# Expert rows summed into x in HBM by accumulating scatters, the last expert's rows and the down biases by products

## The chip, the cores and the metric

One Trainium2 chip, one core. The metric is device time in microseconds (us). Before the change the median of 3 runs is 2022.94 us (2020.0 to 2031.31).

## The reference, cut to what matters

One layer over 512 latent tokens of 1024 channels. The part that the change touches is the mixture of experts at its end and the norm behind it:

```python
logits = (xf @ lp['router_w'] + lp['router_b']).astype(jnp.float32)
top_v, top_e = lax.top_k(logits, TOP_K)            # 4 of 32 experts per token
weights = jax.nn.softmax(top_v, axis=-1)
...                                                # per expert e, on its tokens' rows
return clamped_swiglu(gate, up) @ lp['exp_w_down'][e] + lp['exp_b_down'][e]
...
contrib = yb[dest] * sorted_w[:, None].astype(yb.dtype)
out = jax.ops.segment_sum(contrib, sorted_tok, num_segments=n_tok)
...
x = x + ga2 * moe_ffn(h, lp)                       # then one final RMSNorm
```

`ga2` is a row of 1024 numbers. 512 tokens times 4 choices over 32 experts is 64 rows per expert on average; the kernel gives every expert 128 slots.

## The kernel before, in words

**Routing.** `project_out` ends the mixer: its four tiles of 128 tokens are added to `xn` and written to `d_xn` in HBM. In front of it `merge` makes the operand `mL` on POOL, one subtraction for each of 8 blocks (L1164), and PE waits for each. `route_tile` and `route` then find each token's experts and its slot in each.

**The experts.** `expert_chain` walks a list `seq` in an order written out by hand for PE, ACT and DVE; SP and POOL stand as a scheduler puts them. Round `r` has 12 blocks: 4 of the gate weights of expert r (`pos` 0 to 3), 4 of the down weights of expert r-1 (`pos` 4 to 7) and 4 of the up weights of expert r (`pos` 8 to 11); round 0 has no down part and round 32 nothing else. For each block SP loads 1 MB of weights into one of 6 buffers `raw` (L1462), ACT casts it to `wh` (L1480), DVE takes the remainder `wl` = raw - wh into one of 3 buffers (L1486), and PE multiplies 12 times by 512 columns (L1497, L1498, L1502). The casts run three blocks ahead, the remainders two. `bias_mm` (L1552) opens each gate and each up part, so its rows mark where a round starts.

**The tokens of an expert.** `gather_x` fetches the rows of experts 0 to 3 by products with one-hot matrices on PE (L1523), two experts at a time: the first pair ahead of round 0, the second within round 1. From expert 4 on, `x_rows` gathers 128 rows from `d_h2` by an indirect DMA on POOL (L1532), and `x_turn` transposes them in the round before they are used (L1544). That DMA needs `slots`, the token of each slot. `slot_table` makes it through HBM: 16 indirect scatters of token numbers into one table `d_tab` (L1418), and a load of the table (L1421). What builds the weights and tables runs as the generators `side` and `side_end`, a step behind each block.

**The end.** `y_out` copies an expert's product to `am` (L1589) and ACT's queue writes it to `d_y` (L1591). `finish` gathers each token's four rows back from `d_y` by 16 indirect DMAs on POOL (L1768). For each tile of 128 tokens PE sums two of them by products with diagonal matrices (L1778), the down biases (L1779) and the last expert's rows (L1780); DVE adds the other two (L1782, L1783), multiplies by `ga2` and adds `x` (L1787, L1788); `final_norm` follows and SP writes the tile out (L1810).

Of the kernel before, what the change touches and what calls it, by code (L numbers as in the profile page):

```python
# [19 lines left out]
NLAT = 512  # L20
# [11 lines left out]
NMM = 4  # L32
# [19 lines left out]
NLATE = C_IOTA1 + 128  # L52
# [14 lines left out]
def make_consts():  # L67
# [42 lines left out]
    l[:, C_EB:C_EB + 32] = 1024.0 * np.arange(32)  # L110
    hst = np.zeros((40, 512), np.float32)
# [41 lines left out]
class K:  # L153
# [1030 lines left out]
    def xn_load(self, pool):  # L1184
        self.xn = pool.tile([128, 4, 1024], F32, name="xn")
        self.nc.sync.dma_start(self.xn, self.A["x"].rearrange("(i p) d -> p i d", p=128))
        self.ga1 = self.row_tile(pool, "ga1", self.d_mod[0])

    def project_out(self, c, H, L, tiles=range(4)):
# [10 lines left out]
        if c == 3:  # L1200
            nc.sync.dma_start(self.d_xn[128 * i:128 * i + 128, :], self.xn[:, i, :])
# [117 lines left out]
    def counts(self, pool):  # L1319

        nc = self.nc
        nc.vector.tensor_scalar_add(self.pm, self.pm1, -1.0)
        pc = self.ps.tile([128, 32], F32, name="b1")
        ch = self.moe.tile([128, 4, 32], BF, name="ch")
        nc.vector.tensor_scalar(ch, self.pm, 0.0, None, op0=OP.is_ge)
        for j in range(4):
# [6 lines left out]
    def scratch(self, *shape):  # L1333

        t = self.mraw.tile([128, 2048], F32, name="raw", bufs=RAW)
        n = math.prod(shape)
        names = "abcd"[:len(shape)]
        return t[:, :n].rearrange(f"p ({' '.join(names)}) -> p {' '.join(names)}", **dict(zip(names, shape)))

    def weights(self, pool):  # L1340
# [7 lines left out]
        yield  # L1348
# [17 lines left out]
        nc.vector.tensor_reduce(e_, t, axis=mybir.AxisListType.X, op=OP.add)
        yield

        f = moe.tile([128, 4, 4], F32, name="dsf")
        nc.vector.tensor_sub(f, dst, e_)  # L1370
        big = moe.tile([128, 4, 4], F32, name="big")
# [3 lines left out]
        nc.vector.scalar_tensor_tensor(s, e_, 0.125, f, op0=OP.mult, op1=OP.add)  # L1375
        self.slot = pool.tile([128, 4, 4], I32, name="slot")
        nc.vector.scalar_tensor_tensor(self.slot, big, 8192.0, s, op0=OP.mult, op1=OP.add)
        self.slot_table(pool)
        self.f_, self.e_, self.big = f, e_, big

    def weights_end(self, pool):

        nc = self.nc
        moe = self.moe
        oh = self.oh
        f, e_, big = self.f_, self.e_, self.big
        self.keepR = self.mbL.tile([128, 4096], F32R, name="mL")
        self.keep = self.mb.tile([128, 4096], F32, name="mH")
        wl = moe.tile([128, 4, 4], F32, name="ex")
        nc.vector.tensor_mul(wl, self.wts, oh[:, :, :, NE - 1])  # L1390
        self.wlast = pool.tile([128, 4, 1], F32, name="wlast")
        nc.vector.tensor_reduce(self.wlast.rearrange("p a b -> p (a b)"), wl, axis=mybir.AxisListType.X, op=OP.add)
        yield
        yield from self.down_bias(pool, oh)
        yield
        self.wts2 = pool.tile([128, 4, 4], F32, name="wts2")
        nc.vector.tensor_mul(self.wts2, self.wts, big)
        nc.vector.tensor_sub(self.wts, self.wts, self.wts2)
        yield
        g = moe.tile([128, 4, 4], F32, name="dst")  # L1400
        nc.vector.tensor_scalar_min(g, f, 127.0)
        self.dsti = pool.tile([128, 4, 4], I32, name="dsti")
        nc.vector.scalar_tensor_tensor(g, e_, 0.125, g, op0=OP.mult, op1=OP.add)

        nc.vector.tensor_scalar_min(self.dsti, g, 128.0 * (NE - 1))
        nc.vector.tensor_scalar(g, f, 128.0, -128.0, op0=OP.max, op1=OP.add)
        self.dst2 = pool.tile([128, 4, 4], I32, name="dst2")
        nc.vector.scalar_tensor_tensor(self.dst2, e_, 0.375, g, op0=OP.mult, op1=OP.add)

    def slot_table(self, pool):  # L1410

        nc = self.nc
        tok = pool.tile([128, 4], I32, name="tok")
        lt = self.late[:, C_TOK:C_TOK + 12].rearrange("p (i c) -> p i c", c=3)
        nc.vector.tensor_add(tok.rearrange("p (i c) -> p i c", c=1), lt[:, :, 0:1], lt[:, :, 1:2])
        for i in range(4):
            for k in range(4):
                nc.gpsimd.indirect_dma_start(out=self.d_tab, out_offset=bass.IndirectOffsetOnAxis(ap=self.slot[:, i, k:k + 1], axis=0),  # L1418
                                             in_=tok[:, i:i + 1], in_offset=None, bounds_check=128 * NE - 1, oob_is_err=False)
        self.slots = pool.tile([128, NE], I32, name="slots")  # L1420
        nc.gpsimd.dma_start(self.slots, self.d_tab.rearrange("(e s) a -> s (e a)", s=128))  # L1421

    def down_bias(self, pool, oh):

        nc = self.nc
        moe = self.moe
        w = self.scratch(4, 3, 32)
        u = self.scratch(4, 4, 32)
# [125 lines left out]
    def gate_sig(self, E):  # L1554
# [5 lines left out]
        nc.scalar.activation(sg, sg, AF.Sigmoid, scale=-1.702, bias=self.eps[:, 5:6])  # L1560

# [5 lines left out]
    def up_clamp(self, E):  # L1567
        u = E["u"] = self.moe.tile([128, 1024], F32, name="sg")
        self.nc.vector.tensor_scalar(u, E["up"].rearrange("p a b -> p (a b)"), 7.0, -7.0, op0=OP.min, op1=OP.max)
        E["a"] = self.moe.tile([128, 8, 128], F32, name="am")  # L1570
# [16 lines left out]
    def y_out(self, E):  # L1587
        y = E["y"] = self.moe.tile([128, 1024], F32, name="am")
        self.nc.scalar.copy(y, E["dn"].rearrange("p a b -> p (a b)"))  # L1589
        if E["e"] < NE - 1:  # L1590
            self.nc.scalar.dma_start(self.d_y[128 * E["e"]:128 * E["e"] + 128, :], y)  # L1591

    def expert_bias(self, tmp, m):
# [14 lines left out]
        z = tmp.tile([128, 2, 32], F32, name="selz", bufs=1)  # L1608
# [5 lines left out]
        zi = tmp.tile([128, 32], I32, name="zi", bufs=1)  # L1614
        nc.gpsimd.memset(zi, 0)
        nc.sync.dma_start(self.d_tab.rearrange("(p e) a -> p (e a)", p=128), zi)

    def experts(self):
        self.xf, self.xg = [], {}
        self.nsplit = 0  # L1620
        ET = mybir.EngineType
        with self.tc.manual_schedule(engines={ET.PE, ET.Activation, ET.DVE}):
            y = self.expert_chain()
        self.finish(y)

    def side(self):

        self.counts(self.small)
        yield
        yield from self.weights(self.small)  # L1630

    def side_end(self):

        yield from self.weights_end(self.small)
        yield from self.last_table()

    def expert_chain(self):
# [423 lines left out]
```

## Time and profile before

| | us |
|---|---|
| median of 3 runs | 2022.94 |
| profiled execution, its own time | 2020.75 |
| its span, first to last instruction | 2019.0 |
| PE busy | 1910.1 |
| DVE busy | 1651.7 |
| ACT busy | 1253.7 |
| POOL busy | 328.8 |

The busy times are means over stages that are limited by different things. The expert rounds take the last 1230 us; the chain of waits, the timeline of one engine in a short window and the table of windows say what limits each stretch.

### The profile page before, as it was taken

How to read it: one execution, taken by the hardware profiler on the slowest of the kernel's cores; microseconds unless marked ns; L12 is line 12 of the kernel's file. 1: busy time of each engine (PE TensorE's matmuls, PEld its weight loads, DVE VectorE, ACT ScalarE, POOL GpSimd, SP SyncE). 2: the span in 40 equal slices, each digit the busy share in tenths (PEclk: the TensorE clock that was granted, in tenths of full speed). 3: DMA queues.
4: the chain of work that ended last, by engine and by line, in shares of the span. 5: the costliest groups of instructions: out<-in, count | busy, mean ns of one | idle time of the engine just before them, and what ended most of it. 6: DMA issues, size and time to landing. Idle time of an engine off the chain costs nothing.

```text
span 2019.0 us, 29040 instructions
## 1 busy us (share of the span) xinstructions
PE 1910.1 (95%) x11216; PEld 1500.3 (74%) x11216; DVE 1651.7 (82%) x1760; ACT 1253.7 (62%) x1464; POOL 328.8 (16%) x364
## 2 busy tenths in 40 slices
PE   7999878989999898988999999999999999999986
PEld 4767666667676697876888888888888888888863
DVE  5755786868785567897999999999999999999985
ACT  4522535454545435765777777777777777777762
POOL 0000515353523451220000000000000000000012
PEclk9999989989899998998999999999999999999998
DMA  9665233120111575988999999999999999999984
GB/s 319 205 201 190 85 100 106 56 65 30 52 51 50 181 249 180 343 327 319 365 375 384 372 393 376 373 383 371 387 382 373 385 370 392 370 375 388 369 340 167
DMA packets 154675, 545.11 MB, mean 270 GB/s; under 512 B 14442, under 2 KB 75626, under 8 KB 105379
## 3 DMA queue, kind: packets, MB, share of 16 engines
q1 hardware_dynamic: 140775, 497.97, 66.4%
q0 software_dynamic: 6928, 23.10, 3.4%
q10 hardware_dynamic: 6828, 22.13, 2.7%
q8 instruction: 90, 1.47, 0.3%
q14 instruction: 54, 0.44, 0.1%
HBM read 507.71 MB, written 35.43 MB: 269 GB/s over the span
## 4 chain that ended last, share of the span: by engine, by line
PE 69%; DVE 8%; DMA 3%; issue 2%; POOL 2%; ACT 2%; SPq 0%; POOLq 0%; DVEq 0%; ACTq 0%
PE gp L1497 6%; PE up L1497 6%; PE gp L1498 6%; PE up L1498 6%; PE up L1502 6%; PE gp L1502 6%; PE dn L1502 6%; PE dn L1498 6%; PE dn L1497 6%; PE fill L1091 2%; PE b L1580 1%; PE b L1544 1%; PE mm L870 1%; PE b L1523 1%; PE ch L911 1%
## 5 line engine op out<-in xcount | busy, mean ns | idle before, releaser
L1486 DVE TENSOR_TENSOR wl<-raw,wh 128x2048 fp32r<-128x2048 f32 x384 | 868.8, 2290 | 51.7 <-PE gp L1502 28.3
L1480 ACT CAST wh<-raw 128x2048 fp32r<-128x2048 f32 x384 | 720.8, 1905 | 95.7 <-PE gp L1498 63.5
L1497 PE MATMUL dn<-wh,aH 128*128 128x512 f32 x512 | 207.4, 405 | 0.4 <-ACT aH L1583 0.4
L1497 PE MATMUL gp<-wh,xH 128*128 128x512 f32 x512 | 204.7, 400 | 0.0
L1497 PE MATMUL up<-wh,xH 128*128 128x512 f32 x512 | 204.5, 399 | 0.0
L1498 PE MATMUL dn<-wh,aL 128*128 128x512 f32 x512 | 202.4, 395 | 1.5 <-DVE aL L1584 1.3
L1498 PE MATMUL gp<-wh,xL 128*128 128x512 f32 x512 | 201.9, 394 | 0.0
L1498 PE MATMUL up<-wh,xL 128*128 128x512 f32 x512 | 201.8, 394 | 0.0
L1532 POOL DMA_INDIRECT xg<-d_h,slots x28 | 26.3, 940 | 901.7 <-PE b L1544 893.3
L1502 PE MATMUL dn<-wl,aH 128*128 128x512 f32 x512 | 140.5, 396 | 0.0
L1502 PE MATMUL up<-wl,xH 128*128 128x512 f32 x512 | 139.2, 393 | 0.0
L1502 PE MATMUL gp<-wl,xH 128*128 128x512 f32 x512 | 139.0, 393 | 0.0
L1583 ACT CAST aH<-b 128x512 fp32r<-128x512 f32 x64 | 37.5, 586 | 134.5 <-PE b L1580 134.5
L1498 PEld LDWEIGHTS dn<-wh,aL 128*128 128x128 f32 x512 | 97.2, 190 | 21.8 <-DVE aL L1584 2.6
L1502 PEld LDWEIGHTS gp<-wl,xH 128*128 128x128 f32 x512 | 96.2, 188 | 22.9
L1502 PEld LDWEIGHTS up<-wl,xH 128*128 128x128 f32 x512 | 96.2, 188 | 22.9
L1502 PEld LDWEIGHTS dn<-wl,aH 128*128 128x128 f32 x512 | 97.1, 190 | 21.4
L1498 PEld LDWEIGHTS up<-wh,xL 128*128 128x128 f32 x512 | 96.6, 189 | 21.3
L1498 PEld LDWEIGHTS gp<-wh,xL 128*128 128x128 f32 x512 | 96.5, 189 | 21.1
L1497 PEld LDWEIGHTS dn<-wh,aH 128*128 128x128 f32 x512 | 97.1, 190 | 20.1 <-ACT aH L1583 0.8
L1497 PEld LDWEIGHTS gp<-wh,xH 128*128 128x128 f32 x512 | 96.4, 188 | 20.8
L1497 PEld LDWEIGHTS up<-wh,xH 128*128 128x128 f32 x512 | 96.4, 188 | 20.7
(512 smaller groups left out, 3708.2 us busy)
## 6 DMA issues: line engine op xcount, KB each, us to landing
raw<-in_exp_w_gate_dram SPq DMA_DIRECT2D x128, 1024.0 KB, 7.2
raw<-in_exp_w_up_dram SPq DMA_DIRECT2D x128, 1024.0 KB, 7.7
raw<-in_exp_w_down_dram SPq DMA_DIRECT2D x128, 1024.0 KB, 9.1
raw<-in_w_ada_dram SPq DMA_DIRECT2D x32, 512.0 KB, 4.5
d_y<-am ACTq DMA_DIRECT2D x31, 512.0 KB, 8.8
raw<-in_w_in_dram SPq DMA_DIRECT2D x24, 512.0 KB, 4.1
wa<-in_w_ada_dram SPq DMA_DIRECT2D x7, 1024.0 KB, 11.0
raw<-in_w_in_dram SPq DMA_DIRECT2D x6, 1024.0 KB, 5.5
```

What stands on the lines that cost most here:

```text
L870: nc.tensor.matmul(mm[:, d].rearrange("p a t -> p (a t)"), BK[:, d, ch[d], :], AZ[:, d].rearrange("p a t -> p (a t)"), start=True, stop=True)
L911: nc.tensor.matmul(sp[:, d, :], bk[:, d, :], uv[:, d, :], start=True, stop=True)
L1091: nc.tensor.matmul(ps, a[:, k, :], b[:, k, :], start=(n == 0), stop=(n == 23))
L1480: self.nc.scalar.copy(h, t)
L1486: self.nc.vector.tensor_sub(lo, t, h)
L1497: mm(ps[:, c, :], xH[:, k0 + kk, :], wh[:, cs], start=first and kk == 0, stop=False)
L1498: mm(ps[:, c, :], xL[:, k0 + kk, :], wh[:, cs], start=False, stop=False)
L1502: mm(ps[:, c, :], xH[:, k0 + kk, :], wl[:, cs], start=False, stop=last and kk == 1)
L1523: nc.tensor.matmul(ps[:, c].rearrange("p e s -> p (e s)"), src[:, 2 * q + c, 128 * i:128 * i + 128], oh[:, i].rearrange("p e s -> p (e s)" ...
L1532: self.nc.gpsimd.indirect_dma_start(out=t, out_offset=None, in_=self.d_h2, in_offset=bass.IndirectOffsetOnAxis(ap=self.slots[:, e:e + 1], ...
L1544: nc.tensor.transpose(pt[:, j, :], self.xg[e][:, 128 * k:128 * k + 128], self.ident)
L1583: nc.scalar.copy(aH, pt)
```

## The change

1. `d_xn` becomes `d_acc`, 128 rows longer. Each expert's rows but the last's are scaled by their slot's weight as they are copied (ACT, `y`), multiplied by `ga2` (POOL), and added to `d_acc` by an accumulating indirect scatter (POOL's queue). Empty slots add zero to the spare rows.
2. The slot tables carry token and weight, and are four, one for each of the four choices. They are made ahead of the first remainder `wl` (`places`), and summed within round 1 (`slot_rows`).
3. Only experts 0 and 1 are fetched by products. Experts 2 and 3 are gathered from HBM within round 1; gathers skip empty slots.
4. `finish` adds to the loaded `d_acc` only the bias product and the last expert's product, times `ga2`. The order of the end is written out by hand too.

```diff
-NMM = 4
+NMM = 2
     def xn_load(self, pool):
+        self.nc.gpsimd.dma_start(self.d_acc[NLAT:NLAT + 128, :], self.xn[:, 3, :])
...
-            nc.sync.dma_start(self.d_xn[128 * i:128 * i + 128, :], self.xn[:, i, :])
+            nc.sync.dma_start(self.d_acc[128 * i:128 * i + 128, :], self.xn[:, i, :])
...
+    def places(self, pool):          # was weights(), a step behind each block
...
+        for i in range(4):
+            for k in range(4):
+                nc.gpsimd.indirect_dma_start(out=self.d_tab[k], out_offset=bass.IndirectOffsetOnAxis(ap=slot[:, i, k:k + 1], axis=0),
+                                             in_=tw[:, i, k, :], in_offset=None, bounds_check=128 * NE - 1, oob_is_err=False)
+        self.tab = moe.tile([128, 4, NE, 2], F32, name="y")
+        for j, t in enumerate(self.d_tab):
+            nc.gpsimd.dma_start(self.tab[:, j], t.rearrange("(s e) a -> s e a", e=NE))
...
     def y_out(self, E):
-        y = E["y"] = self.moe.tile([128, 1024], F32, name="am")
-        self.nc.scalar.copy(y, E["dn"].rearrange("p a b -> p (a b)"))
-        if E["e"] < NE - 1:
-            self.nc.scalar.dma_start(self.d_y[128 * E["e"]:128 * E["e"] + 128, :], y)
+        if e == NE - 1:
+            for c in range(2):
+                cs = slice(512 * c, 512 * c + 512)
+                nc.vector.tensor_mul(y[:, cs], E["dn"][:, c, :], self.ga2[:, cs])
+            return
+        nc.scalar.activation(y, E["dn"].rearrange("p a b -> p (a b)"), AF.Copy, scale=self.wslot[:, e:e + 1])
+        nc.gpsimd.tensor_mul(y, y, self.ga2)
+        nc.gpsimd.indirect_dma_start(out=self.d_acc, out_offset=bass.IndirectOffsetOnAxis(ap=self.slotd[:, e:e + 1], axis=0), in_=y, in_offset=None, compute_op=OP.add)
...
-        nc.sync.dma_start(self.d_tab.rearrange("(p e) a -> p (e a)", p=128), zi)
+        for t in self.d_tab:
+            nc.gpsimd.dma_start(t.rearrange("(p e) a -> p (e a)", p=128), zi)
...
+        self.places(self.small)
+        low(0)
+        low(1)
...
+            if r == NE and pos == 4:
+                self.last_part(0, 0)
+                for h in range(2):
+                    self.up_clamp(P, slice(h, h + 1))
+                    self.up_half(P, h)
+                    if h == 0:
+                        self.turn(P, 0)
...
+    def sum_load(self):              # called in round 31 behind y_out
+        for i in range(4):
+            x = self.moex.tile([128, 1024], F32, name=("xH", "xL")[i % 2], bufs=XB)
+            self.nc.gpsimd.dma_start(x, self.d_acc[128 * i:128 * i + 128, :])
...
+    def last_part(self, i, j):
...
+            if j == 0:
+                nc.tensor.matmul(ps, self.wD[:, i, :], self.bD[:, cs], start=True, stop=False)
+            else:
+                nc.tensor.matmul(ps, self.wT[:, i, :], self.ylast[:, cs], start=False, stop=True)
...
+        def add(i):
+            for c in range(2):
+                cs = slice(512 * c, 512 * c + 512)
+                nc.vector.tensor_add(self.xf[i][:, cs], self.xf[i][:, cs], self.pss[i][c])
...
+        add(0); root(0); add(1); scaled(0); root(1); add(3); scaled(1); root(3); add(2); root(2); scaled(3); scaled(2)
```

(`root` is a tile's square sum and root on ACT, `scaled` its division, the product with the norm's weights and the write; the last line is twelve lines in the code.)

The order of instructions at three places, before and after. First POOL in the merge, where it makes `mL` for PE (`xn` adds follow). Before:

```order
L186 TENSOR_TENSOR yaL<-ya,yaH 128x512
L186 TENSOR_TENSOR wh<-raw,wh 128x1024
L1607 TENSOR_TENSOR bias<-biasf,biash 32x512 x2
L1164 TENSOR_TENSOR mL<-ga,mH 128x512 x8
L1199 TENSOR_TENSOR xn<-xn,mo 128x256 x5
```

After (L1191 writes the spare rows, L1639 zeroes a table each):

```order
L1629 TENSOR_TENSOR bias<-biasf,biash 32x512 x2
L1167 TENSOR_TENSOR mL<-ga,mH 128x512 x4
L1191 DMA d_acc<-xn 128x1024
L1637 MEMSET gy 128x64
L1167 TENSOR_TENSOR mL<-ga,mH 128x512
L1639 DMA d_tab_67<-gy 128x64
L1639 DMA d_tab_68<-gy 128x64
L1167 TENSOR_TENSOR mL<-ga,mH 128x512
L1639 DMA d_tab_69<-gy 128x64
L1639 DMA d_tab_70<-gy 128x64
L1167 TENSOR_TENSOR mL<-ga,mH 128x512 x2
```

Five DMA issues stand among the eight subtractions, four of them ahead of the last two. Next DVE where the experts start, from the one-hot matrix of the first pair (L1513) on. Before:

```order
L1513 TENSOR_TENSOR xg<-late,pm_8063 128x1024
L1486 TENSOR_TENSOR wl<-raw,wh 128x2048 x3
L1322 TENSOR_SCALAR pm<-pm_8063 128x128
L1325 TENSOR_SCALAR ch<-pm 128x128
L1329 TENSOR_REDUCE mc<-b_8209 128x1
L1331 CAST maxc<-mc 128x1
```

After, the end of `places` (`slot` and `tw` are what the scatters take):

```order
L1360 TENSOR_REDUCE sm<-ex 128x4
L1361 RECIPROCAL sm<-sm 128x4
L1363 TENSOR_TENSOR wts<-ex,sm 128x16
L1366 TENSOR_TENSOR dsf<-dst,dse 128x16
L1368 TENSOR_SCALAR big<-dsf 128x16
L1371 TENSOR_SCALAR dst<-dsf 128x16
L1372 SCALAR_TENSOR_TENSOR dst<-dse,dst 128x16
L1374 SCALAR_TENSOR_TENSOR slot<-big,dst 128x16
L1377 COPY tw<-wts 128x16
L1379 TENSOR_TENSOR sm<-late 128x4
L1380 TENSOR_SCALAR tw<-sm 128x16
L1493 TENSOR_TENSOR wl<-raw,wh 128x2048 x3
```

Seventeen instructions now stand between the one-hot matrix and the first `wl`: these eleven, and six before them. Last PE behind the last up block, where the last down part (`dn`) begins. Before:

```order
L1502 MATMUL up<-wl,xH 128x512 x4
L1778 MATMUL gp<-raw,mH 128x512 x2
L1580 MATMUL b_16969<-first,am 128x128 x4
L1779 MATMUL gp<-mL 128x512
L1497 MATMUL dn<-wh,aH 128x512
```

After:

```order
L1509 MATMUL up<-wl,xH 128x512 x4
L1793 MATMUL gp<-mL 128x512 x2
L1594 MATMUL b_17012<-first,am 128x128 x4
L1504 MATMUL dn<-wh,aH 128x512
L1505 MATMUL dn<-wh,aL 128x512
```

The products with gathered rows (L1778) no longer stand ahead of the transposes that `dn` needs; a bias product does.

## Rows read from the trace of the kernel before

**Rows 1.** The page, 40 slices of the span: GB/s moved by DMA.

```profile
GB/s 319 205 201 190 85 100 106 56 65 30 52 51 50 181 249 180 343 327 319 365 375 384 372 393 376 373 383 371 387 382 373 385 370 392 370 375 388 369 340 167
```

**Rows 2.** A 36 us window: busy PE, PEld, DVE, ACT, POOL; clock, DMA share, GB/s.

```profile
1140.00:1176.00 36.00, 36.00 (x166) 29.38 (x165) 33.57 (x21) 27.30 (x20) 0.94 (x1) 1.00 0.99 380
```

**Rows 3.** Timeline of PE: start, length; bias products that open gate parts.

```profile
815.17 0.63 PE L1552 MATMUL gp<-bias,selE 128*128 128x512 f32 x2
...
950.00 0.62 PE L1552 MATMUL gp<-bias,selE 128*128 128x512 f32 x2
...
1922.43 0.63 PE L1552 MATMUL gp<-bias,selE 128*128 128x512 f32 x2
```

**Rows 4.** Waits of SP's queue, 950 to 1900 us: total, times, longest.

```profile
SPq L1462 <- DVE wl L1486: 826.3, 317, 4.1
```

**Rows 5.** Timeline of POOL: start, length, count [idle before]; the merge, and two gathers' issues.

```profile
713.72 6.38 POOL L1164 TENSOR_TENSOR mL<-ga,mH 128x512 fp32r<-128x512 f32 x4 [3.40 <-ACT mH L1163]
...
923.45 1.01 POOL L1532 DMA_INDIRECT xg<-d_h,slots  x1 [8.03 <-DMA raw<-in_exp_w_up_dram]
924.77 0.95 POOL L1532 DMA_INDIRECT xg<-d_h,slots  x1 [0.30 <-issue]
```

**Rows 6.** Timeline of POOL: first table scatter, two in a row, the table's load.

```profile
811.66 2.99 POOL L1418 DMA_INDIRECT d_tab<-tok,slot  x1 [32.36 <-DVE tok L1415]
834.25 0.97 POOL L1418 DMA_INDIRECT d_tab<-tok,slot  x1 [5.08 <-DMA d_tab<-tok,slot]
840.23 0.97 POOL L1418 DMA_INDIRECT d_tab<-tok,slot  x1 [5.00 <-DMA d_tab<-tok,slot]
...
913.65 1.77 POOL L1421 DMA_DIRECT2D slots<-d_tab  x1 [5.38 <-DMA d_tab<-tok,slot]
```

**Rows 7.** Timeline of PE in rounds 1 and 3: a one-hot group, and a wait.

```profile
821.20 1.11 PE L1523 MATMUL b<-xg,mH 128*128 128x256 f32 x8
...
932.30 1.09 PE L1544 MATMUL b<-first,xg 128*128 128x128 f32 x4 [9.73 <-DMA xg<-d_h,slots]
```

**Rows 8.** Timeline of DVE: the first three remainders.

```profile
781.08 6.69 DVE L1486 TENSOR_TENSOR wl<-raw,wh 128x2048 fp32r<-128x2048 f32 x3
```

**Rows 9.** The page, DMA issues: count, KB each, us from issue to landing.

```profile
raw<-in_exp_w_down_dram SPq DMA_DIRECT2D x128, 1024.0 KB, 9.1
...
d_y<-am ACTq DMA_DIRECT2D x31, 512.0 KB, 8.8
```

**Rows 10.** Timeline of PE: the first products with a remainder.

```profile
794.08 1.08 PE L1502 MATMUL gp<-wl,xH 128*128 128x512 f32 x4
```

**Rows 11.** Timeline of ACT: the copies of the last two experts' products.

```profile
1950.29 1.00 ACT L1589 COPY am<-dn 128x1024 f32<-128x1024 f32 x1
...
1981.96 1.01 ACT L1589 COPY am<-dn 128x1024 f32<-128x1024 f32 x1 [7.69 <-PE dn L1502]
```

**Rows 12.** Timeline of POOL at the end: products of 128x1024.

```profile
1997.58 2.36 POOL L1807 TENSOR_TENSOR wh<-wh,mH 128x1024 f32<-128x1024 f32 x1 [4.31 <-ACT wh L1806]
2002.36 3.40 POOL L1807 TENSOR_TENSOR wh<-wh,mH 128x1024 f32<-128x1024 f32 x1 [2.42 <-DVE wh L1787]
```

**Rows 13.** Timeline of DVE at the end: one operation twice.

```profile
1993.69 1.29 DVE L1783 SCALAR_TENSOR_TENSOR wh<-raw,wts,wh 128x1024 f32<-128x1024 f32 x1
1998.73 2.29 DVE L1783 SCALAR_TENSOR_TENSOR wh<-raw,wts,wh 128x1024 f32<-128x1024 f32 x1
```

**Rows 14.** Timeline of PE behind the last up part.

```profile
1956.63 1.09 PE L1502 MATMUL up<-wl,xH 128*128 128x512 f32 x4
1964.44 4.12 PE L1778 MATMUL gp<-raw,mH 128*128 128x512 f32 x4 [6.72 <-DMA raw<-d_y,dsti]
...
1969.67 0.50 PE L1497 MATMUL dn<-wh,aH 128*128 128x512 f32 x1 [0.44 <-ACT aH L1583]
```

**Rows 15.** Timeline of DVE at the end: first sum and last division.

```profile
1987.35 1.28 DVE L1782 SCALAR_TENSOR_TENSOR wh<-raw,wts,gp 128x1024 f32<-128x1024 f32 x1 [10.15 <-PE gp L1780]
...
2011.96 1.41 DVE L1809 SCALAR_TENSOR_TENSOR wh<-xL,rs,mH 128x512 f32<-128x512 f32 x2
```

More of the change, by code (lines that the diff above doesn't have):

```diff
@@ L1372, in weights @@
         nc.vector.tensor_scalar(big, f, 128.0, None, op0=OP.is_ge)
         s = moe.tile([128, 4, 4], F32, name="dst")
[L1375 to L1381, printed above, removed]
+        nc.vector.tensor_scalar(s, f, 32.0, None, op0=OP.mult)
@@ new lines, in places @@
+        nc.vector.scalar_tensor_tensor(s, e_, 1.0 / 1024, s, op0=OP.mult, op1=OP.add)
+        slot = pool.tile([128, 4, 4], I32, name="slot")
+        nc.vector.scalar_tensor_tensor(slot, big, 8192.0, s, op0=OP.mult, op1=OP.add)
+        tw = pool.tile([128, 4, 4, 2], F32, name="tw")
+        nc.vector.tensor_copy(tw[:, :, :, 1], self.wts)
+        lt = self.late[:, C_TOK:C_TOK + 12].rearrange("p (i c) -> p i c", c=3)
+        nc.vector.tensor_add(sm, lt[:, :, 0:1], lt[:, :, 1:2])
+        nc.vector.tensor_scalar_add(tw[:, :, :, 0], sm.to_broadcast([128, 4, 4]), 1.0)
@@ L1383, in weights_end, with slot_rows @@
+    def slot_rows(self, pool):
         nc = self.nc
         moe = self.moe
+        v = moe.tile([128, NE, 2], F32, name="slv")
+        nc.vector.tensor_reduce(v, self.tab.rearrange("p j e a -> p e a j"), axis=mybir.AxisListType.X, op=OP.add)
+        self.wslot = pool.tile([128, NE], F32, name="wslot")
+        nc.vector.tensor_copy(self.wslot, v[:, :, 1])
+        em = moe.tile([128, NE], F32, name="slm")
+        nc.vector.tensor_scalar(em, v[:, :, 0], 0.0, None, op0=OP.is_equal)
+        self.slots = pool.tile([128, NE], I32, name="slots")
+        nc.vector.scalar_tensor_tensor(self.slots, em, 1025.0, v[:, :, 0], op0=OP.mult, op1=OP.add)
+        nc.vector.tensor_scalar_add(self.slots, self.slots, -1.0)
+        yield
+        nc.vector.tensor_scalar(em, em, self.late[:, C_SPARE:C_SPARE + 1], None, op0=OP.mult)
+        self.slotd = pool.tile([128, NE], I32, name="slotd")
+        nc.vector.scalar_tensor_tensor(self.slotd, v[:, :, 0], -1.0, em, op0=OP.add, op1=OP.add)
@@ L1405, in weights_end @@
[L1405 to L1428, printed above, removed]
+        w = self.keep[:, 0:384].rearrange("p (i j e) -> p i j e", i=4, j=3)
+        u = self.keep[:, 512:1024].rearrange("p (i k e) -> p i k e", i=4, k=4)
+        b = self.keep[0:96, 1024:2048]
+        self.ga2 = self.keep[:, 2048:3072]
+        nc.sync.dma_start(self.ga2, bcast_rows(self.d_mod[3]))
+        for j in range(3):
+            nc.sync.dma_start(b[32 * j:32 * j + 32, :], self.A["exp_b_down"])
@@ L1565, in gate_mul, with up_clamp @@
         self.nc.vector.scalar_tensor_tensor(gg, g, 7.0, E["sg"], op0=OP.min, op1=OP.mult)
[L1567 to L1570, printed above, removed]
+    def up_clamp(self, E, hs=slice(0, 2)):
+        if "u" not in E:
+            E["u"] = self.moe.tile([128, 1024], F32, name="sg")
+            E["a"] = self.moe.tile([128, 8, 128], F32, name="am")
+        u = E["u"].rearrange("p (a b) -> p a b", a=2)
+        self.nc.vector.tensor_scalar(u[:, hs], E["up"][:, hs], 7.0, -7.0, op0=OP.min, op1=OP.max)
     def up_half(self, E, h):
@@ L1622, in experts @@
         with self.tc.manual_schedule(engines={ET.PE, ET.Activation, ET.DVE}):
-            y = self.expert_chain()
-        self.finish(y)
+            self.expert_chain()
     def side(self):
-        self.counts(self.small)
+        yield from self.sum_start(self.small)
+        yield from self.counts(self.small)
         yield
-        yield from self.weights(self.small)
-    def side_end(self):
-        yield from self.weights_end(self.small)
+        while not self.rows_due:
+            yield
+        yield from self.slot_rows(self.small)
+        yield
+        self.beyond(self.small)
+        yield
         yield from self.last_table()
@@ L1718, in expert_chain @@
                 self.turn(P, 1)
[L1719 to L1725 removed]
+            elif pos in ((6, 8) if r > 1 else (8, 10)) and r < NE and P:
+                self.x_turn(r + 1, int(pos == (8 if r > 1 else 10)), xT)
+            if r == 1 and pos == 4:
+                self.rows_due = True
+            next(side, None)
+            if r == 1 and pos in (4, 5):
+                self.x_rows(pos - 2)
+        self.finish(P)
     def last_table(self):
         nc = self.nc
[L1730 to L1733 removed]
+        self.wT = self.keep[:, 0:512].rearrange("p (a b) -> p a b", a=4)
+        oh = self.keep[:, 512:1024].rearrange("p (a b) -> p a b", a=4)
         io = self.late[:, C_IOTA:C_IOTA + 128].rearrange("p (a s) -> p a s", a=1).to_broadcast([128, 4, 128])
@@ L1759, in finish @@
[L1759 to L1774 removed]
+    def sum_load(self):
+        for i in range(4):
+            x = self.moex.tile([128, 1024], F32, name=("xH", "xL")[i % 2], bufs=XB)
+            self.nc.gpsimd.dma_start(x, self.d_acc[128 * i:128 * i + 128, :])
+            self.xf.append(x)
@@ L1775, in finish @@
+    def finish(self, P):
+        nc = self.nc
+        self.last_part(1, 0)
+        self.last_part(3, 0)
+        self.y_out(P)
+        self.ylast = P["y"]
+        for i in (0, 1, 3):
+            self.last_part(i, 1)
+        self.last_part(2, 0)
+        self.last_part(2, 1)
+        o, rs = {}, {}
+        def add(i):
             for c in range(2):
                 cs = slice(512 * c, 512 * c + 512)
-                for k in range(2):
-                    nc.tensor.matmul(ps[:, c, :], dg[:, k, :], yg[i, k][:, cs], start=(k == 0), stop=False)
@@ L1784, in finish, with root @@
-            n = 1 + (i == 3)
-            for c in range(n):
-                cs = slice(1024 // n * c, 1024 // n * (c + 1))
-                nc.vector.tensor_mul(acc[:, cs], acc[:, cs], self.ga2[:, cs])
-                nc.vector.tensor_add(x[:, cs], x[:, cs], acc[:, cs])
-            self.final_norm(i, self.moe, acc, n)
+                nc.vector.tensor_add(self.xf[i][:, cs], self.xf[i][:, cs], self.pss[i][c])
+        def root(i):
+            o[i] = self.mbW.tile([128, 2048], F32, name="wh", bufs=4)[:, :1024]
+            rs[i] = self.moe.tile([128, 2], F32, name="rs", bufs=2)
+            nc.scalar.activation(o[i], self.xf[i], AF.Square, accum_out=rs[i][:, 0:1])
+            nc.scalar.activation(rs[i][:, 1:2], rs[i][:, 0:1], AF.Sqrt, bias=self.eps[:, 0:1], scale=1.0 / 1024)
@@ new lines, in scaled @@
+        def scaled(i):
+            r = rs[i][:, 0:1]
+            nc.vector.reciprocal(r, rs[i][:, 1:2])
+            rows = self.out[128 * i:128 * i + 128, :]
+            if i == 0:
+                nc.scalar.activation(o[i], self.xf[i], AF.Copy, scale=r)
+                nc.gpsimd.tensor_mul(o[i], o[i], self.fin)
+                nc.sync.dma_start(rows, o[i])
+                return
+            for c in range(2):
+                cs = slice(512 * c, 512 * c + 512)
+                nc.vector.scalar_tensor_tensor(o[i][:, cs], self.xf[i][:, cs], r, self.fin[:, cs], op0=OP.mult, op1=OP.mult)
+                nc.sync.dma_start(rows[:, cs], o[i][:, cs])
@@ L1791, in final_norm @@
+        add(0)
+        root(0)
+        add(1)
+        scaled(0)
+        root(1)
+        add(3)
+        scaled(1)
+        root(3)
+        add(2)
+        root(2)
+        scaled(3)
+        scaled(2)
     def final_norm(self, i, pool, o, n=1):
@@ L1911, in build @@
             self.d_h2 = dram.tile([NLAT, 1024], F32, name="d_h2")
-            self.d_xn = dram.tile([NLAT, 1024], F32, name="d_xn")
-            self.d_y = dram.tile([(NE - 1) * 128 + 1, 1024], F32, name="d_y")
+            self.d_acc = dram.tile([NLAT + 128, 1024], F32, name="d_acc")
             self.d_y2 = dram.tile([NE, 3, 128, 1024], F32, name="d_y2")
-            self.d_tab = dram.tile([NE * 128, 1], I32, name="d_tab")
+            self.d_tab = [dram.tile([128 * NE, 2], F32, name=f"d_tab{j}") for j in range(4)]
             self.d_pm = dram.tile([NE, 128, 4], F32, name="d_pm")
```

182 lines of the change are left out of this document (72 added, 110 removed).

## The prediction, on record before the result

> **What bounds the kernel now.** I read the page's slices first, then a window of one expert round, then PE's timeline at the round starts, then the waits of SP's queue. The slices tell where the rounds run: from about slice 20 on, DMA moves 370 to 392 GB/s [rows 1]. In a window of 36.00 us inside them PE is busy all 36.00 at clock 1.00, while DVE has 33.57, ACT 27.30 and POOL 0.94 [rows 2]; the clock level is 2.4 GHz. The bias products that open gate parts give the period: (1922.43 - 950.00)/27 = 36.02 us for rounds 4 to 31 [rows 3]. So PE sets the period there, and nothing that PE doesn't execute costs anything until it fills another resource. DMA shows a share of 0.99, which would make it the bound as well; but SP's queue waits 317 times, 826.3 us in all, for DVE's `wl` to free a raw buffer [rows 4]. The loads start when a buffer comes free, not when DMA has room, so 380 GB/s is demand and not yet a limit. How far the limit is above it the trace doesn't show; 392 GB/s has been reached [rows 1].
>
> Time is therefore to be had only where PE waits or does extra work: in the merge, in rounds 1 to 3 and behind the last up part.
>
> **The merge.** PE waits for `mL` from POOL. Today four subtractions follow each other in 6.38 us [rows 5], and a gap of 3.40 us ahead of them holds room for the issue of the spare rows' write. The new order puts four more DMA issues ahead of the last two subtractions. Two issues on POOL that follow each other start 924.77 - 923.45 = 1.32 us apart, 1.01 of it the issue and 0.30 between [rows 5]. Four plain ones I take at 1.24 (0.94 and 0.30, 0.94 being near the 0.95 of the second): 5.0 us, less about 0.5 for the gaps they share with the subtractions: +4.5. Bounds: 0 if POOL runs ahead of PE there after all; 4 x (1.77 + 0.30) = +8.3 if each costs what the table's load cost [rows 6].
>
> **Rounds 1 to 3.** They take 950.00 - 815.17 = 134.83 us [rows 3]; three steady rounds are 108.1. The excess is 26.7. It has three parts. 64 one-hot products of the second pair, 8 groups that take PE some 0.95 us each (1.11 with the pipeline's end [rows 7]), are 7.6 us and go. A wait of 9.73 us in round 3 is for the gathered rows of expert 4 [rows 7], which wait for the slot table. The rest, 9.4, is the shorter waits and the slow matmuls behind them. The table is late because its 16 scatters go one by one: POOL waits 5.00 to 5.08 us for the landing of each before it issues the next (0.97), a spacing of 5.98 [rows 6]; the first starts at 811.66 and the load at 913.65.
>
> Afterwards scatter i waits only for scatter i-4, on the same table. Four turns of about 6 us, then four loads of 1.77 and a landing of some 5: 24 + 7 + 5 = 36 us. `places` ends on DVE about 5.4 us behind the present start of the first `wl`, 781.08 [rows 8], at 786.5. The tables are in at about 822. `slot_rows` is wanted at round 1's block 4, some 15 us behind 815.17, about 830: 8 us of slack. The gathers of experts 2 and 3 then leave at blocks 4 and 5 and are wanted behind block 8, some 11 us later. The nearest landing is 8.8 to 9.1 us for 0.5 and 1 MB under load [rows 9]; this fits by 2 us, or stalls PE for 2. Against the excess of 26.7 stand 16 new transposes of experts 2 and 3 in four groups (0.6 each, from 1.09 with the pipeline's end [rows 7]), 2.4 us. Net -24. Bounds: -26.8 with nothing left, and -12 if the first gather lands 10 us late, about the 9.73 of today, and 2 to 4 us of slow matmuls follow.
>
> The 17 operations ahead of the first `wl` cost 5.4 us of DVE. Today that one is ready at 781.08 + 2.23 = 783.3 (a third of 6.69) and PE wants it at 794.08 [rows 8, 10]; afterwards at 788.8. Nothing is late there.
>
> **The steady rounds.** Three engines change, and PE loses nothing and gains nothing. ACT's copy has a scale in place of none, 1.0 us [rows 11] against at most 1.3; ACT has 8.7 us free. POOL gets a product of 128x1024: 2.36 us, or 3.40 where it meets DVE [rows 12], and one scatter issue of 1.0 in place of the one for ACT. What it does to DVE shows at the end of the kernel: an addition of 1.29 us takes 2.29 beside such a product [rows 13]. DVE has 36.00 - 33.57 = 2.43 us free [rows 2], and a `wl` is made 5 us ahead of need: three buffers and a block of 3.0 us leave 8 us from the release to the first product with it, and DVE needs 2.3 and some 0.5 of waiting. A delay of 1 to 2.4 us once per round fits in both. Zero; the bound is the first rival below.
>
> DMA loses half of each gather, 0.26 MB of 0.52, since 64 slots of 128 are empty on average, and d_y's write of 0.52 becomes a sum in HBM, which has to read as well as write: 12.58 + 0.26 + 1.05 = 13.89 MB per round in place of 380 x 36.00 = 13.68, or 386 GB/s. That is under the 392 seen. Zero. The Trainium skill, "HBM Reference", Specifications (TRN2), gives a core about 358 GB/s with both cores of a pair streaming and about 425 alone. By the first, today's 13.68 MB would take 38.2 us, more than the period measured, so the trace rejects it here; by the second 13.89 MB take 32.7 us, an estimate, and the added bytes hide.
>
> **The end.** Let t = 0 where the last up part ends, 1956.63 + 1.09 = 1957.72 [rows 14]. Today PE waits 6.72 for rows gathered from `d_y`, 4.12 goes to four products with them, and `dn` starts at t = 11.95 [rows 14]. It ends at 1981.96 (ACT's copy waits for it [rows 11]), 12.3 us long. The sums start at 1987.35 and DVE ends at 2011.96 + 1.41 = 2013.37 [rows 15], 5.6 us ahead of the span's end, t = 61.3. Afterwards, by halves: clamp and product 1.3 (two of half of 1.29), transposes 0.6, cast 0.5, remainder 0.65, hand-offs 0.4: `dn` starts at 3.5 and ends at 15.8. Its product with `ga2` takes 1.3, PE's last products 0.6: 17.7. DVE then has four sums of 1.3 and three scalings of 1.41, 9.4; the last tile's square and root on ACT 1.5; some ten hand-offs of 0.2: t = 30.6. With the same 5.6 the span ends at 36.2. Saved: 25. The loads of `d_acc` need the last scatter to have landed: copied at 1951.29, multiplied to 1954, issued to 1955, landed at 8.8 behind [rows 9], t = 6; loads of the same 8.8, t = 15, wanted at 17.7. Bounds: -28 with no hand-offs, -17 if scatter and loads take 8 to 11 us more together.
>
> **Sum.** 2020.75 + 4.5 - 24 + 0 - 25 = 1976. The profiled execution is 2.2 us under the median of 2022.94; I say 1977. By the bounds 1966 to 2000.
>
> **Rivals.** (1) POOL's lock isn't absorbed: each round DVE loses the whole 3.40, 33.57 + 3.40 = 36.97 against 36.02, 0.95 x 30 = +28: 2004. For it: the operation that took 2.29 for 1.29 us [rows 13]. Against it: that one lost 1.0 us and not 3.40, and 2.43 are free. (2) Slower: DMA becomes the bound through the accumulation. If a scattered byte occupies the DMA engines like s plain ones, a round has 12.84 + 0.52 s MB. At 392 GB/s the period grows from s = 2.4 on; at s = 3.55 it is 37.5 us and the whole gain (44 us over 30 rounds, 1.5 each) is gone; at s = 4 it is 38.1, +63: 2039. For it: a DMA share of 0.99 already, and no accumulating transfer anywhere in this trace. Against it: SP waits for DVE, not for DMA. (3) The four tables don't take turns: 102 us from 786.5 and 8 for loads, 897 against 830, PE stalls 65: 2042. Against it: four separate tensors.
>
> **How the numbers follow.** Forecast 0.64, rival 1 0.12, rival 2 0.12, rival 3 0.05, mixtures and what I don't see 0.07. A difference of 0.5% (10 us) is about what a measurement tells from none. Faster: the forecast, rival 1 and more than half of the mixtures, 0.81; slower: rivals 2 and 3 less their mild forms, 0.13; 0.06 between. Range 1962 to 2010: the forecast with its bounds, and rival 1; the forecast's own is 1966 to 2000.
>
> **What would show it.** Right: the period between bias products stays 36.0, rounds 1 to 3 take about 111, `dn` starts 3 to 4 us behind the last up part, the end comes some 36 behind it, and PE's waits for `mL` grow by 4 to 5. Wrong: SP's queue waits less for DVE and raw loads land later than 9 us (rival 2); waits of PE for `wl` in every round (rival 1); POOL's table scatters 6 us apart (rival 3); PE waiting for `xg` in round 1 or DVE for `d_acc` at the end (the terms' bounds).

## The result, and the profile after

The changed kernel takes 1991.57 us (median of 4 runs, 1987.12 to 1995.05): 0.984 of before, 95% interval 0.980 to 0.987. 1977 was forecast. The profiled execution took 1995.05 us, its span 1993.3; against the span of before, 2019.0, it saves 25.7, where the sum of the prediction saved 44.5. That execution is the slowest of the four, so the terms below add up to less than the medians' difference of 31.

The first view answers [rows 3]: PE's bias products at the starts of rounds 1, 2, 4 and 31 (start, length, engine, line, tiles, count).

```profile
817.21 0.62 PE L1561 MATMUL gp<-bias,selE 128*128 128x512 f32 x2
...
860.26 0.62 PE L1561 MATMUL gp<-bias,selE 128*128 128x512 f32 x2
...
933.01 0.62 PE L1561 MATMUL gp<-bias,selE 128*128 128x512 f32 x2
...
1918.31 0.62 PE L1561 MATMUL gp<-bias,selE 128*128 128x512 f32 x2
```

Round 1 starts 2.0 us later than before. Rounds 1 to 3 take 115.8 us and not 134.8, round 1 alone 43.1. Rounds 4 to 30 take (1918.31 - 933.01)/27 = 36.49 us each and not 36.02: +12.9 in all. From the start of round 31 to the span's end it is 75.0 us and not 96.6. Sum: 2.0 - 19.0 + 12.9 - 21.6 = -25.7.

A window of one steady round answers [rows 2], with the same columns (busy PE, PEld, DVE, ACT, POOL; clock, DMA share, GB/s):

```profile
1218.00:1254.00 36.00, 36.00 (x164) 28.86 (x163) 34.97 (x20) 26.83 (x20) 8.43 (x3) 1.00 1.00 369
```

DVE has 1.03 us free where it had 2.43, with nothing new to do: the groups show why (busy time, mean ns of one, idle before them; first `wl` before the change, then `wl` and POOL's product after it).

```profile
L1486 DVE TENSOR_TENSOR wl<-raw,wh 128x2048 fp32r<-128x2048 f32 x384 | 868.8, 2290 | 51.7 <-PE gp L1502 28.3
...
L1493 DVE TENSOR_TENSOR wl<-raw,wh 128x2048 fp32r<-128x2048 f32 x384 | 928.0, 2461 | 1.9 <-issue 1.0
...
L1612 POOL TENSOR_TENSOR y<-y,mH 128x1024 f32<-128x1024 f32 x31 | 135.8, 4381 | 152.0 <-ACT y L1611 152.0
```

`wl` took 2290 ns before and had 51.7 us of idle time ahead of it; now 1.9. POOL's product takes 4.38 us, nearly twice the 2.36 of [rows 12]. Where it runs, three `wl` take 8.9 us. The next three views show POOL, then DVE over the same time, then PE's weight loads one round part later:

```profile
1147.18 4.50 POOL L1612 TENSOR_TENSOR y<-y,mH 128x1024 f32<-128x1024 f32 x1 [2.21 <-ACT y L1611]
1151.96 3.35 POOL L1613 DMA_INDIRECT d_acc<-y,slotd  x1 [0.28 <-POOL y L1612]
```

```profile
1149.33 8.89 DVE L1493 TENSOR_TENSOR wl<-raw,wh 128x2048 fp32r<-128x2048 f32 x3
1158.15 1.21 DVE L1584 TENSOR_SCALAR sg<-up 128x1024 f32<-128x1024 f32 x1
...
1163.61 0.70 DVE L1598 TENSOR_TENSOR aL<-b,aH 128x512 fp32r<-128x512 f32 x1
```

```profile
1163.73 0.19 PEld L1504 LDWEIGHTS dn<-wh,aH 128*128 128x128 f32 x1
1164.37 0.19 PEld L1505 LDWEIGHTS dn<-wh,aL 128*128 128x128 f32 x1 [0.45 <-DVE aL L1598]
```

The delay doesn't die out. DVE goes from `wl` without a break to `sg` and on to `aL`, and the first `dn` products wait for `aL` in every round. PE's own busy time hides it (36.00 of 36.00); the waits of its weight loads show it (1000 to 1900 us: total, times, longest):

```profile
PEld dn L1505 <- DVE aL L1598: 10.8, 25, 0.5
```

The kernel before has no such wait in that stretch.

The merge, answering [rows 5]: four table issues between the last four subtractions.

```profile
714.00 1.72 POOL L1167 TENSOR_TENSOR mL<-ga,mH 128x512 fp32r<-128x512 f32 x1 [0.52 <-ACT mH L1166]
715.68 1.11 POOL L1639 DMA_DIRECT2D d_tab<-gy  x2
716.81 1.28 POOL L1167 TENSOR_TENSOR mL<-ga,mH 128x512 fp32r<-128x512 f32 x1
718.03 1.09 POOL L1639 DMA_DIRECT2D d_tab<-gy  x2
719.13 2.63 POOL L1167 TENSOR_TENSOR mL<-ga,mH 128x512 fp32r<-128x512 f32 x2
```

Two issues take 1.11 us, 0.55 each.

The slot table, answering [rows 6]: scatters on POOL (the first, the seventh, the eighth, the last), the last of four loads, and the first gather.

```profile
787.77 2.83 POOL L1383 DMA_INDIRECT d_tab<-tw,slot  x1 [6.87 <-DVE tw L1380]
...
803.18 1.28 POOL L1383 DMA_INDIRECT d_tab<-tw,slot  x1 [3.22 <-DMA d_tab<-tw,slot]
804.76 3.03 POOL L1383 DMA_INDIRECT d_tab<-tw,slot  x1 [0.30 <-issue]
...
824.62 0.97 POOL L1383 DMA_INDIRECT d_tab<-tw,slot  x1 [0.30 <-issue]
...
831.76 0.54 POOL L1387 DMA_DIRECT2D y<-d_tab  x1 [0.97 <-DMA d_tab<-tw,slot]
839.55 2.35 POOL L1540 DMA_INDIRECT xg<-d_h,slots  x1 [7.25 <-DVE slots L1401]
```

The landings are hidden nearly always. The issues now set the pace: most take 1 to 3 us, 1.9 on average, where 0.97 was counted. The gathered rows come late, and PE goes on at 0.63 us per product, spaced 0.43, before it returns to 0.40 and 0.23; the granted clock is 1.00 from 844 to 848 us, where PE stops, and 0.50, the lower level of 1.2 GHz, from 850.5 to 853.5 (PE, round 1):

```profile
848.00 0.63 PE L1553 MATMUL b<-first,xg 128*128 128x128 f32 x4 [2.52 <-DMA xg<-d_h,slots]
...
852.10 0.63 PE L1504 MATMUL up<-wh,xH 128*128 128x512 f32 x1
852.53 0.63 PE L1505 MATMUL up<-wh,xL 128*128 128x512 f32 x1
```

The end, answering [rows 14]: PE from the last up block on.

```profile
1953.03 1.09 PE L1509 MATMUL up<-wl,xH 128*128 128x512 f32 x4
...
1958.45 0.50 PE L1504 MATMUL dn<-wh,aH 128*128 128x512 f32 x1 [0.68 <-ACT aH L1597]
...
1959.85 0.63 PE L1505 MATMUL dn<-wh,aL 128*128 128x512 f32 x1
...
1971.30 1.09 PE L1509 MATMUL dn<-wl,aH 128*128 128x512 f32 x4
...
1973.17 1.99 PE L1795 MATMUL gp<-am,mH 128*128 128x512 f32 x4
```

With t = 0 at 1954.12, `dn` starts at 4.3, ends at 18.3, and the span ends at 39.2.

### The profile page after: what moved, and what is told of

It reads as the page before. It is cut to its first block, busy times and chain, and to the rows that moved or that the text cites. A ratio compares the mean times of both kernels' runs of the same rounds, so it can differ in the third digit from the quotient of the medians.

```text
span 1993.3 us, 28998 instructions
## 1 busy us (share of the span) xinstructions
PE 1903.4 (95%) x11136; PEld 1485.9 (75%) x11136; DVE 1703.8 (85%) x1764; ACT 1246.2 (63%) x1441; POOL 567.5 (28%) x423
## 4 chain that ended last, share of the span: by engine, by line
PE 69%; DVE 7%; issue 3%; POOL 3%; DMA 2%; ACT 1%; SPq 0%; POOLq 0%; DVEq 0%; ACTq 0%
PE dn L1505 6%; PE dn L1504 6%; PE dn L1509 6%; PE up L1504 6%; PE up L1505 6%; PE up L1509 6%; PE gp L1505 6%; PE gp L1504 6%; PE gp L1509 6%; PE fill L1094 2%; PE b L1594 1%; PE b L1553 1%; PE mm L873 1%; PE ch L914 1%; PE acc L166 1%
## 5 line engine op out<-in xcount | busy, mean ns | idle before, releaser
L1493 DVE TENSOR_TENSOR wl<-raw,wh 128x2048 fp32r<-128x2048 f32 x384 | 928.0, 2461 | 1.9 <-issue 1.0
L1540 POOL DMA_INDIRECT xg<-d_h,slots x30 | 35.1, 1171 | 687.0 <-PE b L1553 679.1
L1505 PE MATMUL dn<-wh,aL 128*128 128x512 f32 x512 | 206.4, 403 | 0.3 <-DVE aL L1598 0.2
L1612 POOL TENSOR_TENSOR y<-y,mH 128x1024 f32<-128x1024 f32 x31 | 135.8, 4381 | 152.0 <-ACT y L1611 152.0
L1509 PEld LDWEIGHTS dn<-wl,aH 128*128 128x128 f32 x512 | 96.6, 189 | 24.1 <-DVE wl L1493 1.1
L1509 PEld LDWEIGHTS up<-wl,xH 128*128 128x128 f32 x512 | 96.6, 189 | 22.7
L1505 PEld LDWEIGHTS up<-wh,xL 128*128 128x128 f32 x512 | 96.8, 189 | 21.6
L1505 PEld LDWEIGHTS gp<-wh,xL 128*128 128x128 f32 x512 | 96.4, 188 | 21.6
```

What stands on the lines that cost most here:

```text
L1493: self.nc.vector.tensor_sub(lo, t, h)
L1505: mm(ps[:, c, :], xL[:, k0 + kk, :], wh[:, cs], start=False, stop=False)
L1509: mm(ps[:, c, :], xH[:, k0 + kk, :], wl[:, cs], start=False, stop=last and kk == 1)
L1612: nc.gpsimd.tensor_mul(y, y, self.ga2)
```

## The experiments

**What lengthens the steady rounds.** Theory L says POOL's product, D the accumulating scatter. The period is the time from one gate part's bias products to the next, taken over rounds 4 to 30.

```
e1: -nc.gpsimd.tensor_mul(y, y, self.ga2)
e2: -...in_=y, in_offset=None, compute_op=OP.add)   +...in_=y, in_offset=None)
e3: +nc.gpsimd.tensor_mul(y, y, self.ga2)           (a second time)
e4: -nc.scalar.activation(y, dn, AF.Copy, scale=self.wslot[:, e:e + 1])
    -nc.gpsimd.tensor_mul(y, y, self.ga2)
    +nc.vector.scalar_tensor_tensor(y, dn, self.wslot[:, e:e + 1], self.ga2, op0=OP.mult, op1=OP.mult)
```

> The product of each expert's rows with ga2 on POOL is left out (the sums then lack ga2). In the changed kernel the period between gate parts is 36.49 us against 36.02 before. Theory L: POOL's product of 4.4 us keeps DVE out, the wl beside it take longer (three in 8.9 us instead of 6.8), DVE has no slack left and aL comes late for the first dn products. Then without the product three wl take 6.8 us again, PE's weight loads don't wait for aL, the period falls to 36.0 to 36.2 and the time to 1979 to 1985 us. Theory D: the accumulating scatter slows the rounds through DMA. Then the period stays at 36.5 and the time at 1991.

Measured: 1985.77 us, period 36.23, each just above L's range and far from D's. `wl` (the group) has its idle time back:

```profile
L1493 DVE TENSOR_TENSOR wl<-raw,wh 128x2048 fp32r<-128x2048 f32 x384 | 865.3, 2285 | 45.1 <-PE gp L1509 28.2
```

> The scatter writes rows where the changed kernel adds them (the sums are then wrong); product and issue on POOL stay. Theory D (the accumulation costs): period back to 36.0 to 36.2, time 1979 to 1985 us, the landing of the scatter shorter than 13.8 us. Theory L (POOL's product costs): period stays at 36.5, time 1991, even if the landing gets shorter.

Measured: 1992.87 us, period 36.49. D falls: the accumulation isn't the cause.

> POOL multiplies by ga2 twice (the sums then hold ga2 squared): the suspected cost doubled. Theory L: DVE loses some 2 us more per round; it is busy 35.0 of 36.0 now, so about 37.1 of it are wanted, and the period becomes 37.0 to 38.5, the time 2007 to 2050 us. Theory D: period 36.5, time 1991, since POOL has 20 us free in each round.

Measured: 2079.63 us, period 39.31. The direction is L's, the size is above the range: 2.8 us per round for 4.3 us more of POOL. The loss has moved, too: DVE is busy 38.32 of 39.31 us (window 1218 to 1257.31), and PE now waits openly for DVE's `am`, 23 times between 1000 and 1900 us, 44.5 us in all.

> DVE computes product times slot weight times ga2 in one operation from dn, in place of ACT's scaled copy and POOL's product; the scatter stays. Theory L: no lock, DVE wants 33.57 + 1.24 = 34.8 us per round, wl takes 2.29 throughout, the period is 36.0 to 36.3 and the time 1979 to 1987 us. Theory D: period 36.5, time 1991. A third possibility: any 1.2 us more on DVE makes aL late, whoever causes it, and the period stays near 36.4.

Measured: 1981.40 us (0.981 of before, 0.978 to 0.983), period 36.22, DVE busy 34.43 of 36.00. DVE can do the whole work itself at less cost than beside POOL. From 1000 to 1900 us no weight load waits for `aL`, and the four `dn` blocks tell where the gain is: from its first product to the first of the next block, the first takes 3.41 us in the changed kernel and 3.15 here (medians of 25 rounds), the other three the same to 0.01. L holds for 0.27 us per round; 0.21 stay.

**The 0.21 that stay.**

```
e7, on e4: -indirect_dma_start(out=self.d_acc, ..., compute_op=OP.add)
           +nc.scalar.dma_start(self.d_acc[NLAT:NLAT + 128, :], y)
e8, on e4: empty slots gather row 0, no bounds_check
e9, on before: +self.mraw.tile([128, 72], F32, name="pad")   (288 bytes, first in the pool)
```

> As the fourth experiment, but each expert's rows are written to 128 spare rows from ACT's queue, without a scatter (the sums then lack the experts' rows). In every variant without POOL's product the period is 36.22 us, 0.21 above the 36.02 of before: the products with wh are 1 to 4 ns further apart in all blocks. Theory S (the scatter's many descriptors slow PE's operands): period 36.0. Rival P (where the tiles lie in the on-chip memory, or the gathers, does it): 36.22.

> As the fourth experiment, but empty slots gather row 0 instead of being skipped, so each gather moves 128 rows again (their weight is zero). If the skipping of rows makes the 0.21 us per round, the period is 36.0; if DMA were near its limit it would grow beyond 36.22, since 0.26 MB per round come back; else 36.22. The time is then 1976 to 1986 us.

Measured: 1977.70 and 1980.06 us, both with a period of 36.22. Neither scatter nor gather does it, and DMA has room for the 0.26 MB more per round of e8.

> The kernel before with 288 bytes of unused memory per partition ahead of the weight buffers, so that raw, wl, xH and xL lie at the addresses that they have in the changed kernel; every instruction is the same. Theory P (the 0.21 us per round that stay without scatter, product and skipped rows come from where the tiles lie): the period becomes 36.2 instead of 36.02, the time 2025 to 2030 us. Rival Q (the period goes with something else in the changed program, its instructions or its transfers): 36.02 and the time of before within 3 us.

Measured: 2026.05 us, 1.0022 of before (1.0008 to 1.0037), period 36.22, by PE's rows at the starts of rounds 4 and 31:

```profile
953.43 0.62 PE L1552 MATMUL gp<-bias,selE 128*128 128x512 f32 x2
...
1931.48 0.62 PE L1552 MATMUL gp<-bias,selE 128*128 128x512 f32 x2
```

The kernel before, moved by 288 bytes, has the period of the changed one without its product, and the medians of its twelve blocks agree with e4's to 0.01 us. Theory P holds.

**Rounds 1 to 3.**

```
e5: scatters to self.d_tab[0] instead of self.d_tab[k]
e6, on e4: round 1 x_turn at pos 9, 11 (was 8, 10); tables zeroed by nc.sync
```

One execution says little about a few us of round 1: it took 43.1 us in the changed kernel, 40.0 in e2 and 39.2 in e4, with the same table and gathers in all three.

> The changed kernel, but all 16 scatters of the slot table go to one of the four tables, so that each waits for the one before; the sum over the tables is the same. Theory T (the four tables take turns, which is what brings rounds 1 to 3 from 134.8 to 115.8 us): the scatters are some 6 us apart, the table is in at about 787 + 96 + 6 = 889 instead of 837, PE waits some 50 us in round 1, and the time is 2035 to 2050 us. Rival (POOL's issues set the pace, 2.4 us apart, and the landings are hidden anyway): 1991 us and the same round 1.

Measured: 2018.23 us, round 1 66.2. PE waits 25.3 us for `wl`, behind DVE's wait for the table. The scatters (POOL, numbers 2, 3, 10 and 11) are 6 to 8 us apart at first and 2.4 later:

```profile
795.72 1.00 POOL L1383 DMA_INDIRECT d_tab<-tw,slot  x1 [5.09 <-DMA d_tab<-tw,slot]
804.03 2.50 POOL L1383 DMA_INDIRECT d_tab<-tw,slot  x1 [7.31 <-DMA d_tab<-tw,slot]
...
842.26 0.97 POOL L1383 DMA_INDIRECT d_tab<-tw,slot  x1 [1.40 <-DMA d_tab<-tw,slot]
844.66 0.97 POOL L1383 DMA_INDIRECT d_tab<-tw,slot  x1 [1.44 <-DMA d_tab<-tw,slot]
```

The turns are worth about 23 us of round 1. The stall is half of what was expected, since each landing comes in 1.4 us instead of 5 once PE stands; that the weight loads stand with it is the likely reason, not shown.

> As the fourth experiment (DVE makes the product with weight and ga2), and in round 1 the transposes of expert 2 stand behind blocks 9 and 11 instead of 8 and 10; the four tables are zeroed from SP's queue instead of POOL's. Theory: PE's wait of 2.5 us for the gathered rows of expert 2 and the slow products behind it (12 at 0.43 us, some 2.4 us lost) go, round 1 takes 36.3 to 38 us instead of 39.2 to 43.1; PE waits for mL 1.6 us in all instead of 3.9. With the fourth experiment's 1981.4 that is 1974 to 1980 us. Rival (xL of expert 2 then comes late for round 2, or SP's queue holds the zeroing back until the scatters wait for it): round 2 or round 1 gets longer by as much, 1980 us or more.

Measured: 1983.45 us, round 1 43.6: no gain over e4. The rows are in time now, but the last expert's table, a block ahead, waits for DVE. PE in round 1:

```profile
844.09 0.88 PE L1769 MATMUL b<-first,mH 128*128 128x128 f32 x4 [3.59 <-DVE mH L1765]
```

Its wait for `mL` is 1.6 us, as expected, against 3.9 in the changed kernel; but e4, which zeroes the tables on POOL, has 2.2, so 0.6 is what the move is shown to save.

**Toward a better version.**

```
e10, on e6: last_table 8 blocks later; +self.mraw.tile([128, 24], F32, name="pad")   (96 bytes)
e11, on the changed kernel: the same 96 bytes alone
e12, on e10: slot_rows a block later, x_rows at pos 6, 7, x_turn at 10, 11;
             +self.moe.tile([128, 32], F32, name="pad2")   (128 bytes, moves aH and aL)
```

> As the sixth experiment, and the last expert's table (its products wait for DVE) is made 8 blocks later, in round 2; 96 bytes are left free ahead of the weight buffers, so that the tiles of the rounds lie as before by multiples of 128 bytes. Theory: PE's wait of 3.6 us for DVE's mH and the slow products behind it go, round 1 takes 36.3 to 38 us instead of 43.6: 1975 to 1979 us with the period of 36.22, and by theory P, with 36.02, 1970 to 1974 us. Rival (PE waits in round 1 for the gathered rows all the same): round 1 stays above 40 us and the time at 1980 or above.

Measured: 1972.57 us, period 35.78, below that of before, and round 1 still 42.7: PE waits 3.9 us for `wl` behind DVE's wait of 6.1 for the table. The time lies in the range of theory P by luck: round 1 gained nothing, and the period fell further than to 36.02.

> The changed kernel with 96 bytes left free ahead of the weight buffers, every instruction the same. If the loss per round has two parts that add, POOL's product (0.27 us) and the place of the tiles (36.22 without the product at the changed kernel's addresses, 35.78 at these), the period falls from 36.49 to 36.05, some 0.44 x 27 = 12 us, to 1978 to 1982 us, and the wait of the weight loads for aL stays. If the two don't add (PE's faster products only wait longer for DVE, which is busy 35.0 of 36.0), the period stays above 36.2.

Measured: 1989.29 us, period 36.40. The parts don't add: PE alone could do 35.78, and DVE beside POOL's product holds it at 36.40. The weight loads wait for `aL` (1000 to 1880 us), and in a window PE is no longer full:

```profile
PEld dn L1505 <- DVE aL L1598: 12.6, 24, 0.6
...
1218.00:1254.00 36.00, 35.84 (x164) 28.90 (x163) 35.08 (x21) 27.07 (x20) 8.58 (x3) 1.00 0.99 368
```

> As the tenth experiment (1972.57 us, period 35.78, round 1 42.74, where PE waited 3.9 us for wl behind DVE's wait for the slot table), with the table's sums on DVE one block later, the gathers of experts 2 and 3 two blocks later, the transposes of expert 2 behind blocks 10 and 11, and 128 bytes free ahead of sg, so that aH and aL too lie at the same remainder by 256 as wh. Theory: round 1 takes 36 to 39 us, 4 to 6 us less; the products of the down parts come 0.05 us per block closer together, as those of gate and up did, so the period is 35.6 and the time 1962 to 1968 us. Rivals: the gathered rows come late instead (round 1 stays above 41); the down parts don't change (period 35.78).

Measured: 1960.73 us, 0.969 of before (0.967 to 0.972), the best, and just under the range. Round 1 takes 36.2, the period is 35.64 (PE, rounds 1, 2, 4 and 31):

```profile
811.66 0.71 PE L1561 MATMUL gp<-bias,selE 128*128 128x512 f32 x2
...
847.84 0.70 PE L1561 MATMUL gp<-bias,selE 128*128 128x512 f32 x2
...
921.44 0.62 PE L1561 MATMUL gp<-bias,selE 128*128 128x512 f32 x2
...
1883.81 0.63 PE L1561 MATMUL gp<-bias,selE 128*128 128x512 f32 x2
```

## Why the prediction was right or wrong

- **Direction and range: right.** The time lies in 1962 to 2010 and in the forecast's own 1966 to 2000. The two gains came where they were placed, in rounds 1 to 3 and at the end, each smaller than said. The forecast's range doesn't vouch for the steady rounds: its bounds were added up from the other three terms, with nothing lost there.
- **The steady rounds: wrong, 0 against +12.9, the largest miss.** The step that failed is "A delay of 1 to 2.4 us once per round fits in both". The product was priced by [rows 12 and 13], from an end of the kernel where DVE had other operations; beside `wl` it took 4.4 us and cost DVE 2.1 (12 `wl` per round at 2461 ns and not 2290). DVE's spare time and the 5 us ahead of need were counted for `wl`, but `sg` and `aL` stand behind `wl` on the same engine with no such lead. That is rival 1's mechanism at a smaller price: 0.27 us per round (e1, e4) of its 0.95. The scatter's issue takes 3.3 us of POOL, not 1.0, and that costs nothing: e1 keeps it.
- **No rival held the other 0.21 us per round.** It is a matter of where the tiles lie (e9).
- **DMA: right.** SP's queue still waits for DVE's `wl`, 827.2 us between 950 and 1900 (826.3 before), and the extra bytes hide (e2, e7, e8). The 358 GB/s that the Trainium skill, "HBM Reference", Specifications (TRN2), gives a core while both of a pair stream is again exceeded, with 369 in the window; its 425 for a core streaming alone is not reached in any run here.
- **Rounds 1 to 3: mechanism right (e5), -24 against -19.0.** The mis-sized term is the table: 16 scatters that start 2.5 us apart on average, 36.9 us from the first to the last, not four turns of 6, so it was read at 837 and not 822. The 8 us of slack became a wait of 2.5 and slow products. In the profiles of e1, e2, e4, e7 and e8 the term is -19.5 to -23.1, so part of the miss is that execution's. e12 shows the rest was to be had: round 1 at 36.2.
- **The merge: right place, +4.5 against about +2.3** (PE's waits for `mL`, 3.9 us for 1.6; e1 and e4, with the same order, have 2.2, a cost of 0.6). The start of round 0, 793.30 for 791.75, is no measure: it moves by more between executions, 794.87 in e9 with the instructions of before. A plain issue on POOL takes 0.55 us, not 0.94; the price was from an indirect one.
- **The end: -25 against -22.1** (from the last up part, 61.3 us to 39.2; the -21.6 holds round 31 as well, 0.5 longer). `dn` started 0.8 us later than said and took 13.9 us for 12.3: PE came out of its wait at 0.63 per product, with a granted clock of 0.50 from 1959.7 to 1963, as in round 3 before (0.50 from 932 to 936.5). PE's last products take 1.9 us per tile, not 0.6.

## What to carry to other kernels

A spare engine is not free when it shares something with a full one: price its work by what the neighbour's operation takes beside it, and follow the delay along the neighbour's program to the operation with the least lead, not to the one with the most. When a period moves by half a per cent with the same instructions, shift the buffers before looking for a cause in the program.

## What was not expected of the hardware

The place of tiles in on-chip memory changes PE's period by 1.2% (36.22 in e6, 35.78 in e10). No trace shows an address: the remainders below are added up from the tiles that the kernels allocate, and the edits fix only the steps between them (288, 96 and 128 bytes). With `xH` at a remainder of 96, 128 and 224 by 256 bytes, a plain block of gate or up takes 2.78, 2.79 and 2.72 us (before, e9 and the changed kernel, e10); `wh` lies at 224 throughout. Moving `aH` and `aL` from 96 to 224 (e12) brings a `dn` block with transposes behind it from 2.79 to between 2.72 and 2.75. Most of e9's 0.21 us lies in the `dn` blocks too, 0.13 of it, and its shift takes `aH` and `aL` away from 224, where they lie before. Shortest is the time where the expert weights (`wh`) and the token rows (`xH`, `aH`) have the same remainder. Whether that is the rule, or another property of those addresses, wasn't tried.
